# A decoder block with product-key experts: gathered rows for 224 tokens instead of 192, routing four heads at a time, squares of finished rows in SBUF

## The chip, the cores and the metric

The kernel runs on one NeuronCore of a Trainium2 chip, in one launch. The metric is the device time of that launch in microseconds (us). The kernel before took 3629.07 us (median of three runs, 3625.85 to 3631.55). A difference below about 0.2% (some 7 us) can hardly be told from none.

The engines are named as the profile names them: PE multiplies matrices, PEld is its weight load, DVE and ACT work on tiles elementwise, POOL (GpSimd) issues the indirect DMAs, SP issues the plain DMAs. A DMA of either kind runs on the core's 16 DMA engines.

## The reference

512 tokens of width 2048 pass a mixer (a projection to 10240 columns, a short convolution, stick-breaking attention, two gates, an output projection), and then an expert layer, in which the work around the change lies:

```python
q = einsum("btd,dq->btq", rmsnorm(x), wq).reshape(b, t, 8, 2, 128)
scores = einsum("bthsc,snc->bthsn", q, subkeys)         # 8 heads, 2 halves, 128 keys
top_s, top_i = top_k(scores, 16)
cand_s = top_s[..., 0, :, None] + top_s[..., 1, None, :]
cand_i = top_i[..., 0, :, None] * 128 + top_i[..., 1, None, :]
sel_s, sel_pos = top_k(cand_s, 16); sel_i = take_along_axis(cand_i, sel_pos)
act = gelu(einsum("td,thkd->thk", x, u[sel_i])) * softmax(sel_s)
out = rmsnorm(x + einsum("thk,thkd->td", act, v[sel_i]))
```

Each token chooses 8 x 16 = 128 of 16384 experts, and u and v have one row of 2048 floats (8 KB) for each expert.

## The kernel before

The tokens are handled in two halves of 256. For each half come the mixer (`mixer`, `outproj`), normalization and transposition (`chain`) and the scores (`queries`, in two halves of four heads each). Every weight comes from memory in pieces of 128x1024 floats (`whalf`): SP issues its load, ACT rounds it to `whi`, DVE subtracts to get `wlo` (L133, L134), and three matmuls use the pair (`mm3`, L164 to L166). So each piece costs DVE one `wlo`, and two pieces are one unit of the loops that follow.

The expert layer is done in two ways at once.

- **Dense.** For the last ND = 320 tokens `dense` multiplies all 16384 experts: `up` (uT, 128 units) and `down` (vT, 128 units), in 16 chunks of eight units each. Unwanted experts have gate 0; `gates` makes the gate planes. A dense unit is 48 matmuls with 320 columns, 12288 of them in all. The first eight chunks of `up` come first, then eight chunks of `down`, then both in turn.
- **Gathered.** For the first G0 = 192 tokens `gather_tile` fetches rows of u and v: one round is one indirect DMA of 128 rows (1 MB) into a `row` buffer and one DVE pass over 128x2048 (L696 for u, L703 for v). The first 128 tokens take 128 rounds for u and 128 for v. The next 64 tokens lie twice on the 128 partitions, half of the slots each, so they take 64 and 64, and their two partial sums are added at the end (`finish`, L757, L758). There are four `row` buffers (`ROWS`), shared with other work; while v is summed, the sum holds one of them.

`pump` hands out the rounds along the units of PE's work: at rates of about one per unit at first, and in the dense part so that they run out ten units before its end (`even`, L1038). The generator `route` (top 16 of the scores, candidates, gates) is likewise spread over units, by the costs that it yields. When the scores of all eight heads of the first 128 tokens have been routed, the gathering starts (L972).

This is only the order in which the program is written. The Tile scheduler then places every instruction on its engine by a timeline of its own; the engines take their instructions strictly in the order that results. DVE's gather passes keep their order among themselves (`PIN`, L691) and may be put late between the `wlo` of the weights.

A finished 128-token tile gets its norm in `finish_rows`: two squares of 1024 columns, written to a PSUM tile of the same pool as the accumulators of `down` (`rms_scale`, L193), then the scale and the store. The last chunk of `down` transposes its results through PSUM (`tr`, one buffer) in 24 steps, adds them to rows of x (L845), and the final norm follows (L888 to L897). The `row` buffers for those rows are asked for when the gathering is over (L877 to L882).

## Time and profile before

| what | value |
|---|---|
| runs, median (lowest to highest) | 3629.07 us (3625.85 to 3631.55) |
| the profiled execution: span | 3629.1 us, nothing else is listed around it |
| PE busy, share of the span | 3535.7 us, 97% |
| DVE | 2833.4 us, 78% |
| ACT | 1621.6 us, 45% |
| POOL | 644.8 us, 18% |
| data moved | 1056.10 MB, mean 291 GB/s |
| PE's share of the chain that ended last | 73% |

The busy shares are means over stages with different limits, so the stretches of the program have to be read one by one: the columns of the windows below give each engine's busy time in a stretch with the number of its instructions, then PE's granted clock, the busy share of the DMA engines and the rate that they moved.

### The profile page before, as it was taken

How to read it: one execution, taken by the hardware profiler on the slowest of the kernel's cores; microseconds unless marked ns; L12 is line 12 of the kernel's file. 1: busy time of each engine (PE TensorE's matmuls, PEld its weight loads, DVE VectorE, ACT ScalarE, POOL GpSimd, SP SyncE). 2: the span in 40 equal slices, each digit the busy share in tenths (PEclk: the TensorE clock that was granted, in tenths of full speed). 3: DMA queues.
4: the chain of work that ended last, by engine and by line, in shares of the span. 5: the costliest groups of instructions: out<-in, count | busy, mean ns of one | idle time of the engine just before them, and what ended most of it. 6: DMA issues, size and time to landing. Idle time of an engine off the chain costs nothing.

```text
span 3629.1 us, 63343 instructions
## 1 busy us (share of the span) xinstructions
PE 3535.7 (97%) x25347; PEld 3420.6 (94%) x25347; DVE 2833.4 (78%) x4022; ACT 1621.6 (45%) x2277; POOL 644.8 (18%) x520
## 2 busy tenths in 40 slices
PE   9999999999999999889999999999999999999998
PEld 8999999798888999779999999999999999999997
DVE  6555557558988888788999886888887888888885
ACT  5444445445545543554337773333333333333334
POOL 0000000000234222012121111221122322322220
PEclk9999999999999999999999999999999999999998
DMA  5556666663788899899889889899988988889884
GB/s 194 170 176 219 214 216 216 198 193 127 267 306 332 335 344 356 313 331 344 295 324 334 309 317 364 326 358 337 341 328 327 358 328 336 325 338 349 326 319 150
DMA packets 297815, 1056.10 MB, mean 291 GB/s; under 512 B 36464, under 2 KB 109296, under 8 KB 243568
## 3 DMA queue, kind: packets, MB, share of 16 engines
q1 hardware_dynamic: 242224, 649.38, 51.3%
q0 software_dynamic: 55296, 402.68, 28.9%
q8 instruction: 199, 3.26, 0.3%
q14 instruction: 96, 0.79, 0.1%
HBM read 999.98 MB, written 51.38 MB: 290 GB/s over the span
## 4 chain that ended last, share of the span: by engine, by line
PE 73%; DVE 3%; DMA 2%; issue 2%; ACT 1%; POOL 0%; SPq 0%; DVEq 0%; ACTq 0%; POOLq 0%
PE pj L166 13%; PE pj L164 13%; PE pj L165 13%; PE z L164 9%; PE z L165 9%; PE z L166 9%; PE pj L668 2%; DVE wlo L134 1%; PE z L434 1%; PE tr L416 1%; DVE row L696 1%; DMA wraw<-in_w_mix 1%; DMA row<-in_u,idx 1%; PE z L397 0%; DMA gt<-gd 0%
## 5 line engine op out<-in xcount | busy, mean ns | idle before, releaser
L133 ACT ACTIVATE whi<-wraw 128x1024 fp32r<-128x1024 f32 x827 | 874.2, 1059 | 1229.3 <-PE pj L165 726.4
L134 DVE TENSOR_TENSOR wlo<-wraw,whi 128x1024 fp32r<-128x1024 f32 x827 | 1009.2, 1224 | 415.3 <-ACT whi L133 409.5
L166 PE MATMUL pj<-xhi,wlo 128*128 128x256 f32 x2560 | 719.7, 282 | 11.3 <-DVE wlo L134 11.1
L164 PE MATMUL pj<-xhi,whi 128*128 128x256 f32 x2560 | 721.6, 282 | 6.7 <-ACT whi L133 4.7
L165 PE MATMUL pj<-xlo,whi 128*128 128x256 f32 x2560 | 720.5, 282 | 0.0
L164 PE MATMUL pj<-dxhi,whi 128*128 128x320 f32 (+1 forms) x2304 | 710.0, 308 | 2.8 <-ACT whi L133 2.6
L166 PE MATMUL pj<-dxhi,wlo 128*128 128x320 f32 (+1 forms) x2304 | 704.1, 307 | 4.5 <-DVE wlo L134 4.5
L165 PE MATMUL pj<-dxlo,whi 128*128 128x320 f32 (+1 forms) x2304 | 705.8, 307 | 0.0
L164 PE MATMUL z<-ahi,whi 128*128 128x320 f32 x2048 | 631.0, 309 | 4.0 <-ACT z L193 2.9
L165 PE MATMUL z<-alo,whi 128*128 128x320 f32 x2048 | 631.5, 309 | 2.4 <-DVE alo L134 2.4
L166 PE MATMUL z<-ahi,wlo 128*128 128x320 f32 x2048 | 629.6, 309 | 1.8 <-DVE wlo L134 1.8
L166 PEld LDWEIGHTS pj<-xhi,wlo 128*128 128x128 f32 x2560 | 480.0, 188 | 21.5 <-DVE wlo L134 16.1
L164 PEld LDWEIGHTS pj<-xhi,whi 128*128 128x128 f32 x2560 | 481.7, 188 | 12.6 <-ACT whi L133 6.1
L165 PEld LDWEIGHTS pj<-xlo,whi 128*128 128x128 f32 x2560 | 481.4, 188 | 6.7 <-issue 5.3
L685 POOL DMA_INDIRECT row<-in_v,idx x192 | 286.7, 1493 | 1063.8 <-DVE row L703 448.9
L703 DVE SCALAR_TENSOR_TENSOR row<-row,gact 128x2048 f32<-128x2048 f32 x192 | 450.5, 2346 | 19.3 <-DMA row<-in_v,idx 19.3
L696 DVE SCALAR_TENSOR_TENSOR row<-row,gx 128x2048 f32<-128x2048 f32 x192 | 438.4, 2287 | 26.0 <-DMA row<-in_u,idx 25.0
L685 POOL DMA_INDIRECT row<-in_u,idx x192 | 290.8, 1515 | 857.8 <-DVE row L696 213.0
L166 PEld LDWEIGHTS pj<-dxhi,wlo 128*128 128x128 f32 x2304 | 433.3, 188 | 5.6 <-DVE wlo L134 5.6
L164 PEld LDWEIGHTS pj<-dxhi,whi 128*128 128x128 f32 x2304 | 434.5, 189 | 3.2 <-ACT whi L133 2.9
L165 PEld LDWEIGHTS pj<-dxlo,whi 128*128 128x128 f32 x2304 | 434.2, 188 | 0.0
L133 ACT ACTIVATE whi<-spare 128x1024 fp32r<-128x1024 f32 x197 | 208.8, 1060 | 414.8 <-PE z L165 263.8
(232 smaller groups left out, 5019.3 us busy)
## 6 DMA issues: line engine op xcount, KB each, us to landing
wraw<-in_w_in SPq DMA_DIRECT2D x320, 512.0 KB
wraw<-in_uT SPq DMA_DIRECT2D x187, 512.0 KB
wraw<-in_vT SPq DMA_DIRECT2D x128, 512.0 KB
spare<-in_vT SPq DMA_DIRECT2D x128, 512.0 KB
spare<-in_uT SPq DMA_DIRECT2D x69, 512.0 KB
wraw<-in_w_mix SPq DMA_DIRECT2D x64, 512.0 KB
wraw<-in_w_out SPq DMA_DIRECT2D x64, 512.0 KB
wraw<-in_wq SPq DMA_DIRECT2D x64, 512.0 KB
```

The costliest lines, as they stand in the source:

```text
L133: nc.scalar.activation(hi, src, AF.Copy)
L134: nc.vector.tensor_tensor(lo, src, hi.bitcast(F32), OP.subtract)
L164: nc.tensor.matmul(acc, shi, mhi, start=first, stop=False)
L165: nc.tensor.matmul(acc, shi, mlo, start=False, stop=False)
L166: pe_last[0] = nc.tensor.matmul(acc, slo, mhi, start=False, stop=last)
L416: nc.tensor.matmul(yps[hs, q0:], kv[j // 2][1][:, j % 2, hs], e[:, seg(j)], start=j == 0, stop=j == last, skip_group_check=True)
L434: nc.tensor.matmul(z[:, c], stat.bitcast(F32), src[:, c], start=False, stop=True, skip_group_check=True)
L668: behind(nc.tensor.matmul(gp[:, t * P:t * P + P], oh[:, t, 0], oh[:, t, 1], start=True, stop=True))
L685: ins = nc.gpsimd.indirect_dma_start(out=g, out_offset=None, in_=tab, in_offset=bass.IndirectOffsetOnAxis(ap=idx[0:np_, s:s + 1], axis=0))
L696: pin(nc.vector.scalar_tensor_tensor(g, g, 1.0, gx, OP.mult, OP.mult, accum_out=hid[:, s:s + 1]))
L703: pin(nc.vector.scalar_tensor_tensor(acc[0:np_], g, act[:, s:s + 1], acc[0:np_], OP.mult, OP.add))
```

## The change

The gathered tokens become 224 and the dense ones 288. The 96 tokens of the second tile are gathered in two parts: 64 tokens twice on the partitions, as before, and then 32 tokens four times (32 rounds for u, 32 for v), whose four partial sums are added in two steps. Routing works on four heads at a time, in the order tile 0, tile 1, tile 0, tile 1; the gathering starts when the first four heads of tile 0 are done. The squares of finished rows are eight passes of 256 columns with an SBUF tile for the unused output. Line numbers of the kernel after are some 2 to 17 higher.

```diff
-NG2 = 64
+SEGS = ((0, 0, 128), (1, 0, 64), (1, 64, 32))
+NG2 = 96
@@ rms_scale
-        ss = pool.tile([P, 2], F32, name="ss", bufs=2)
-        for c in range(2):
-            junk = ztile()
-            nc.scalar.activation(junk, x[:, c * 1024:c * 1024 + 1024], AF.Square, accum_out=ss[:, c:c + 1])
-        return rms_inv(ss)
+        ss = pool.tile([P, 8], F32, name="ss", bufs=2)
+        for c in range(8):
+            junk = pool.tile([P, 256], F32, name="junk", bufs=1)
+            nc.scalar.activation(junk, x[:, c * 256:c * 256 + 256], AF.Square, accum_out=ss[:, c:c + 1])
+        nc.vector.tensor_reduce(ss[:, 0:1], ss, AX.X, OP.add)
+        return rms_root(ss)
@@ route
-    def route(pool, tile_no, st):
-        ls = pool.tile([P, 2, 8, 2, 16], F32, name="ls", bufs=1)
+    def route(pool, tile_no, hh, st):
+        hs = slice(4 * hh, 4 * hh + 4)
+        ls = pool.tile([P, 2, 4, 2, 16], F32, name="ls", bufs=1)
...
+        if tile_no * P < G0:
+            ef = pool.tile([P, 64], F32, name="fa", bufs=1)
+            nc.vector.scalar_tensor_tensor(ef, flat[:, 0, fs], 128.0, flat[:, 1, fs], OP.mult, OP.add)
+            idx = late[1].tile([P, 64], I32, name=f"idx_{hh}", bufs=2)
+            nc.vector.tensor_copy(idx, ef)
+            st["idx"][tile_no].append(idx)
@@ gather_tile
+                while s // idx[0].shape[1] >= len(idx):
+                    yield
@@ gather
+        for tile_no, p0, n in SEGS:
+            R = P // n
+            rows = slice(tile_no * P + p0, tile_no * P + p0 + n)
...
+            def load_acc(t):
+                if R > 1:
+                    nc.vector.memset(t, 0.0)
+                nc.sync.dma_start(t[0:n], x2d[rows])
+
+            def finish(t):
+                m = P // 2
+                while m >= n:
+                    o = row()
+                    nc.sync.dma_start(o[0:m], t[m:2 * m])
+                    nc.vector.tensor_tensor(t[0:m], t[0:m], o[0:m], OP.add)
+                    m //= 2
+                finish_rows(t, rows, final_gain())
@@ pump, routing, background
-    rounds = 2 * P + (2 * (P // (P // NG2)) if NG2 else 0)
+    rounds = sum(2 * n for _, _, n in SEGS)
-        for tt in range(2):
-            yield from route(rts[0], 2 * h + tt, st)
+        for hh in range(2):
+            for tt in range(2):
+                yield from route(rts[0], 2 * h + tt, hh, st)
-        due = min(due, 0.0) + (SIDE_A0 if not st["routes"][0] else SIDE_A if unit < GATES_AT else SIDE_G)
+        due = min(due, 0.0) + (SIDE_A0 if not st["idx"][0] else SIDE_A if unit < GATES_AT else SIDE_G)
-        if st["routes"][0] and what != "half":
+        if st["idx"][0] and what != "half":
```

What the scheduler makes of this stands in the order of each engine's instructions. First DVE, in the last two chunks of the dense part, where the kernel before ends its gathering; `row<-row,gact` is a round of v, `row,hid<-row,gx` one of u, `wlo` a piece of weights, `hd`, `ahi`, `alo` expert activations, and L758 adds the two partial sums.

```order
L703 SCALAR_TENSOR_TENSOR row<-row,gact 128x2048
L134 TENSOR_TENSOR wlo<-spare,whi 128x1024
L774 TENSOR_TENSOR hd<-hd,gt 128x320
L703 SCALAR_TENSOR_TENSOR row<-row,gact 128x2048
L134 TENSOR_TENSOR wlo<-wraw,whi 128x1024
L134 TENSOR_TENSOR alo<-hd,ahi 128x320
L134 TENSOR_TENSOR wlo<-spare,whi 128x1024
L774 TENSOR_TENSOR hd<-hd,gt 128x320
L134 TENSOR_TENSOR alo<-hd,ahi 128x320
L758 TENSOR_TENSOR row<-row 64x2048
L134 TENSOR_TENSOR wlo<-wraw,whi 128x1024
L197 TENSOR_TENSOR ss<-ss 128x1
```

Behind the last round there 17 `wlo` follow before the program ends. The same engine in the kernel after, at the last `wlo` of the program (L136 there; L854 is the addition of a product of `down`, L773 adds partial sums):

```order
L136 TENSOR_TENSOR wlo<-wraw,whi 128x1024
L708 SCALAR_TENSOR_TENSOR row,hid<-row,gx 128x2048
L854 TENSOR_TENSOR dacc<-z,dacc 128x576
L708 SCALAR_TENSOR_TENSOR row,hid<-row,gx 128x2048 x2
L854 TENSOR_TENSOR dacc<-z,dacc 128x576
L708 SCALAR_TENSOR_TENSOR row,hid<-row,gx 128x2048 x6
L765 MEMSET row 128x2048
L708 SCALAR_TENSOR_TENSOR row,hid<-row,gx 128x2048
L712 TENSOR_TENSOR gact<-gact,gate_34114 128x32
L715 SCALAR_TENSOR_TENSOR row<-row,gact 128x2048 x32
L773 TENSOR_TENSOR row<-row 64x2048
L773 TENSOR_TENSOR row<-row 32x2048
```

The 24 final steps follow these rows. So 42 rounds, ten of u and all 32 of v of the last part, stand behind the last `wlo`, and 39 of them behind the last addition of a product; counted over the dense part, 271 rounds stand among its 512 `wlo`, where 267 stood before.

Second PE at its end, before: `z` are products of `down`, `tr` are transposes.

```order
L166 MATMUL z<-ahi,wlo 128x320
L843 MATMUL tr<-ident,dacc 64x128 x2
L164 MATMUL z<-ahi,whi 128x320
L165 MATMUL z<-alo,whi 128x320
L166 MATMUL z<-ahi,wlo 128x320
```

And after:

```order
L166 MATMUL z<-ahi,whi 128x288
L167 MATMUL z<-alo,whi 128x288
L168 MATMUL z<-ahi,wlo 128x288
L859 MATMUL tr<-ident,dacc 128x128 x4
L859 MATMUL tr<-ident,dacc 32x128 x2
```

Before, 13 of the 24 steps' transposes stand among the products of the last chunk; after, all 24 stand behind the last product.

Third DVE where the gathering starts, before (MAX, MAX_INDEX and MATCH_REPLACE are routing):

```order
L546 MAX ls<-ttmp 128x8 x2
L547 MAX_INDEX ls<-ls,ttmp 128x8 x2
L696 SCALAR_TENSOR_TENSOR row,hid<-row,gx 128x2048
L545 MATCH_REPLACE ttmp<-ls,row 128x128 x2
L403 SCALAR_TENSOR_TENSOR row<-z,row 128x896
```

And after:

```order
L409 SCALAR_TENSOR_TENSOR row<-z,row 128x896
L708 SCALAR_TENSOR_TENSOR row,hid<-row,gx 128x2048
L551 MATCH_REPLACE ttmp<-sv,spare 128x64 x2
L435 TENSOR_TENSOR sums<-row,sums 128x256
L136 TENSOR_TENSOR wlo<-wraw,whi 128x1024
```

Counted in `wlo`, the first round stands behind the 289th piece of weights before and the 268th after; by the 320th there are 19 rounds before and 33 after, by the 512th (the start of the dense part) 117 and 135.

## Rows read from the trace of the kernel before

**Rows 1.** The page: busy time of the engines.
```profile
PE 3535.7 (97%) x25347; PEld 3420.6 (94%) x25347; DVE 2833.4 (78%) x4022; ACT 1621.6 (45%) x2277; POOL 644.8 (18%) x520
```

**Rows 2.** Stretches: from:to, length, busy time by engine, clock, DMA share, GB/s.
```profile
460.00:480.00 20.00, 20.00 (x172) 20.00 (x171) 11.65 (x15) 8.69 (x11) 0.00 (x0) 1.00 0.66 198
797.50:1051.20 253.70, 243.29 (x1792) 216.87 (x1790) 223.92 (x569) 136.31 (x161) 51.20 (x56) 1.00 0.64 223
1716.00:1954.00 238.00, 234.62 (x1605) 233.82 (x1604) 233.29 (x564) 106.76 (x157) 47.41 (x31) 0.99 0.87 313
1954.00:2238.00 284.00, 279.66 (x1998) 278.87 (x1997) 226.29 (x438) 183.46 (x378) 43.36 (x33) 0.99 0.90 331
2238.00:2697.00 459.00, 453.71 (x3073) 450.58 (x3073) 391.13 (x369) 159.23 (x185) 91.93 (x65) 1.00 0.92 339
2697.00:2812.00 115.00, 112.13 (x765) 111.87 (x764) 92.57 (x84) 43.65 (x54) 25.28 (x17) 1.00 0.88 331
2812.00:3489.00 677.00, 677.00 (x4615) 676.58 (x4614) 555.41 (x507) 238.65 (x290) 186.63 (x113) 1.00 0.89 336
3489.00:3605.00 116.00, 115.96 (x796) 115.47 (x795) 84.20 (x93) 47.64 (x78) 9.50 (x7) 1.00 0.64 232
3605.00:3630.00 25.00, 6.53 (x24) 2.50 (x22) 11.88 (x32) 9.48 (x28) 0.00 (x0) 0.57 0.32 105
```

**Rows 3.** PE's timeline: the first and the last dense matmul (start, length).
```profile
1716.40 0.31 PE L164 MATMUL pj<-dxhi,whi 128*128 128x320 f32 x1
...
3604.86 0.31 PE L166 MATMUL z<-ahi,wlo 128*128 128x320 f32 x1
```

**Rows 4.** The page's costliest groups: busy, mean ns, idle before and its releaser.
```profile
L164 PE MATMUL z<-ahi,whi 128*128 128x320 f32 x2048 | 631.0, 309 | 4.0 <-ACT z L193 2.9 <-DVE dacc L838 0.7
L703 DVE SCALAR_TENSOR_TENSOR row<-row,gact 128x2048 f32<-128x2048 f32 x192 | 450.5, 2346 | 19.3 <-DMA row<-in_v,idx 19.3
L696 DVE SCALAR_TENSOR_TENSOR row<-row,gx 128x2048 f32<-128x2048 f32 x192 | 438.4, 2287 | 26.0 <-DMA row<-in_u,idx 25.0 <-DVE wlo L134 1.0
```

**Rows 5.** Stretches in which the DMA engines were fullest.
```profile
2200.00:2250.00 50.00, 46.24 (x304) 45.72 (x303) 35.32 (x36) 18.16 (x26) 10.17 (x7) 0.97 1.00 374
1250.00:1450.00 200.00, 196.11 (x1645) 194.14 (x1644) 163.03 (x174) 81.91 (x102) 44.07 (x30) 1.00 0.95 349
```

**Rows 6.** POOL's timeline: two issues of a gather.
```profile
1069.08 0.97 POOL L685 DMA_INDIRECT row<-in_u,idx  x1 [5.15 <-issue]
...
1111.94 1.68 POOL L685 DMA_INDIRECT row<-in_u,idx  x1 [6.92 <-DVE row L696]
```

**Rows 7.** DVE's timeline: the passes over those two gathers.
```profile
1075.67 2.29 DVE L696 SCALAR_TENSOR_TENSOR row<-row,gx 128x2048 f32<-128x2048 f32 x1 [6.66 <-DMA row<-in_u,idx]
...
1119.26 2.29 DVE L696 SCALAR_TENSOR_TENSOR row<-row,gx 128x2048 f32<-128x2048 f32 x1 [0.85 <-DMA row<-in_u,idx]
```

**Rows 8.** SP's and DVE's timelines: adding the partial sums, then scaling the finished rows.
```profile
3536.68 0.48 SPq L757 DMA_DIRECT2D row<-row  x1
...
3542.09 2.28 DVE L758 TENSOR_TENSOR row<-row 64x2048 f32<-64x2048 f32 x1
...
3550.28 2.35 DVE L725 SCALAR_TENSOR_TENSOR row<-row,ss 128x2048 f32<-128x2048 f32 x1
```

**Rows 9.** DVE's timeline: steps of the final rows once PE's products are done.
```profile
3614.30 0.42 DVE L845 TENSOR_TENSOR row<-tr,row 128x256 f32<-128x256 f32 x1
...
3615.69 0.41 DVE L845 TENSOR_TENSOR row<-tr,row 64x256 f32<-64x256 f32 x1
...
3618.85 0.41 DVE L845 TENSOR_TENSOR row<-tr,row 128x256 f32<-128x256 f32 x1
```

More of the change, by code (lines that the diff above doesn't have):

```diff
@@ L547, in top16 @@
         nc.vector.max_index(ti[:, 8:16], tv[:, 8:16], tmp)
-    def route(pool, tile_no, st):
-        ls = pool.tile([P, 2, 8, 2, 16], F32, name="ls", bufs=1)
+    def route(pool, tile_no, hh, st):
+        hs = slice(4 * hh, 4 * hh + 4)
+        ls = pool.tile([P, 2, 4, 2, 16], F32, name="ls", bufs=1)
         tv, ti = ls[:, 0], ls[:, 1].bitcast(U32)
-        for _ in range(8):
+        for _ in range(4):
             while not st["topk"][tile_no]:
@@ L728, in gather @@
     def gather(routes):
-        idx = routes[0][0]
-        yield from gather_tile(
-            late[1], P, P, idx, st["gate"],
-            lambda t: nc.sync.dma_start(t, xn2d[0:P]),
-            lambda t: nc.sync.dma_start(t, x2d[0:P]),
-            lambda t: finish_rows(t, slice(0, P), final_gain()))
-        if not NG2:
-            return
-        S = P // (P // NG2)
-        idx, eg = routes[1]
-        idx2 = late[1].tile([P, S], I32, name="idx2")
-        gate2 = late[1].tile([P, S], F32, name="gate2")
@@ L741, in gather @@
-        for r in range(P // NG2):
-            ps_, ss = slice(r * NG2, r * NG2 + NG2), slice(r * S, r * S + S)
-            nc.sync.dma_start(idx2[ps_], idx[0:NG2, ss])
-            nc.sync.dma_start(gate2[ps_], eg[0:NG2, 2, ss])
-        def load_x(t):
-            for r in range(P // NG2):
-                nc.sync.dma_start(t[r * NG2:r * NG2 + NG2], xn2d[P:G0])
-        def load_acc(t):
-            nc.vector.memset(t, 0.0)
-            nc.sync.dma_start(t[0:NG2], x2d[P:G0])
-        def finish(t):
-            for r in range(1, P // NG2):
-                o = row()
-                nc.sync.dma_start(o[0:NG2], t[r * NG2:r * NG2 + NG2])
-                nc.vector.tensor_tensor(t[0:NG2], t[0:NG2], o[0:NG2], OP.add)
-            finish_rows(t, slice(P, G0), final_gain())
@@ L761, in gather, with load_x @@
-        yield from gather_tile(late[1], P // NG2 * NG2, S, idx2, gate2, load_x, load_acc, finish)
+        for tile_no, p0, n in SEGS:
+            R = P // n
+            rows = slice(tile_no * P + p0, tile_no * P + p0 + n)
+            idx, gate = st["idx"][tile_no], st["gate"]
+            if R > 1:
+                src, eg = routes[tile_no]
+                idx = [late[1].tile([P, n], I32, name=f"idx{n}")]
+                gate = late[1].tile([P, n], F32, name=f"gate{n}")
+                for r in range(R):
+                    ps_, ss = slice(r * n, r * n + n), slice(r * n, r * n + n)
+                    c = r * n % 64
+                    nc.sync.dma_start(idx[0][ps_], src[r * n // 64][p0:p0 + n, c:c + n])
+                    nc.sync.dma_start(gate[ps_], eg[p0:p0 + n, 2, ss])
+            def load_x(t):
+                for r in range(R):
+                    nc.sync.dma_start(t[r * n:r * n + n], xn2d[rows])
+            def load_acc(t):
+                if R > 1:
+                    nc.vector.memset(t, 0.0)
[8 more added lines that the diff above has]
+                finish_rows(t, rows, final_gain())
+            yield from gather_tile(late[1], P, n, idx, gate, load_x, load_acc, finish)
@@ L897, in dense @@
                 nc.sync.dma_start(out[G0 + c:G0 + c + n, half * 1024:half * 1024 + 1024], xs)
-    st = {"routes": [None] * 4}
+    st = {"routes": [None] * 4, "eg": [None] * 4, "idx": [[] for _ in range(4)]}
     credit = 0.0
```

81 lines of the change are left out of this document (41 added, 40 removed).

## The prediction

> **What bounds the kernel now.** I read the page's busy times first, then the stretches, then the timelines at the end. PE is busy 3535.7 of 3629.1 us [rows 1], and the stretches show that this is no average over mixed stages: from 2812 to 3489 us PE is busy for all of 677 us at granted clock 1.00, while DVE has 555 of 677 and the DMA engines 0.89 [rows 2]. There only PE can set the time, and a change that shortens its matmuls is paid out until the next engine is full. How near that engine is differs by stretch: DVE has 233.3 of 238 us from 1716 to 1954, and the DMA engines 0.92 from 2238 to 2697 [rows 2]. The dense part lasts from 1716.4 to 3604.9 us [rows 3], and after the last product only 24.2 us are left to the end at 3629.1. The profiled span equals the median of the runs (3629.07) within 0.1 us, so the sum is made on the span and not scaled.
>
> **Dense matmuls, the gain.** A matmul with 320 columns takes 677 / 4615 = 146.7 ns from start to start, one with 256 columns 20.00 / 172 = 116.3 ns [rows 2]. 288 lies half way: 131.5 ns, 15.2 ns less. 12288 of them make 187 us: 47 in the first 3072 (1716 to 2238), 47 in the next (2238 to 2697), 93 in the rest. What of it is kept depends on the neighbours. DVE's order has almost as many rounds per piece of weights as before (271 in the dense part against 267), so DVE's and the DMA engines' work stays nearly what it is and has to fit into less time.
>
> - 1716 to 2238: in the first half DVE is busy 233.3 of 238 us, and routing of the other tokens, one-hot planes and 63 rounds against 62 are still its work. I grant 3 us there. In the second half (DVE 226 of 284) PE's 24 us are free. Sum -27, bounds 0 and -47.
> - 2238 to 2697: the DMA engines moved 339 GB/s x 459 us = 155.6 MB, and nearly the same must be moved. The best 50 us of the trace have 374 GB/s at a full share of 1.00 [rows 5]; at that rate it takes 416 us, PE would need 412. DVE, busy 391 us now, loses only a tenth of its passes over 320 and 640 columns, and would stand at some 380 of 412 (an estimate). Two engines so near to full do not fit without gaps; I take 423 us, -36, bounds -10 and -47.
> - The rest, 2697 to 3605: 115 x 331 + 677 x 336 + 116 x 232 = 292.5 MB; at 374 GB/s 782 us, and PE needs 907 - 93 = 814. From 1250 to 1450 us PE kept 98% beside a DMA share of 0.95 [rows 5], so little is lost. PE's 4.0 us of waits at the products of `down`, 2.9 of them for the squares in PSUM [rows 4], go with the SBUF tile (-3), and the 13 pairs of transposes that leave the last chunk, 26 at about the 116 ns of a narrow matmul, give -3 here and come back below. -99 at best; I take -88, bound -60.
>
> The Trainium skill, *DMA: Bandwidth & Descriptors* (Specifications), gives about 358 GB/s as a core's share of the memory. The 374 GB/s over 50 us above exceed it, so I do not use it as a wall; by it the second stretch would take 435 us and the sum below come out 12 us higher. The same skill's *TensorE: Matmul & The Clock Gate* (Back-to-back issue gap) has N / 2.4 + 2.5 ns per matmul, 135.8 for 320 columns, where the rows have 146.7; by the page the step to 288 is worth 13.3 ns, an estimate 24 us lower in all and some 12 us after the stretches' own limits.
>
> **Before the dense part, a loss.** From 797 to 1051 us DVE is busy 223.9 of 253.7 us and PE 243.3 [rows 2]. By the order, 33 rounds instead of 19 now stand before the 320th `wlo`: 14 x (2.29 + 0.08) = 33 us more for DVE. Routing in half-width pieces doubles some 22 small instructions per tile (+5), and some of routing moves behind the 320th `wlo` (-5). 257 us no longer fit into 253.7; at 97% busy it takes 265: +12 us, bounds -4 (all of it finds gaps, and 32 tokens fewer need planes) and +33. The DMA engines have room there (0.64). The start of gathering cannot help by itself: what stands behind it is paced by PE's units.
>
> **Behind the last product, the new cost.** Here the order decides, not the pacing in the program. Before, the last round has 17 `wlo` behind it, so the addition of the partial sums, the norm and 13 of the 24 final steps lie beside products. After, the scheduler has put 42 rounds behind the last `wlo`, 39 of them behind the last addition of a product, and all 24 final steps behind those. PE is done by then and hides nothing. Step by step:
>
> - 7 rounds of u at 2.37 us [rows 4] and a memset: 19 us.
> - 32 rounds of v. One buffer's cycle is issue to pass, 1075.67 - 1069.08 = 6.6 and 1119.26 - 1111.94 = 7.3 us [rows 6, 7], two cases in which DVE waited for the data, and the pass itself, 2.35 [rows 4]: 9.0 to 9.7. Three of the four buffers are left beside the sum, so 3.0 to 3.2 us a round. DVE alone would need 2.35 (75 us in all); two buffers only, 4.7 (150). The weights no longer load, so I take 3.0: 96 us.
> - Two additions of partial sums, each behind its own DMA: before, at most 3542.09 - 3536.68 = 5.4 us from the issue to the addition, and 2.28 for that [rows 8]. At most 15; I take 13.
> - From the end of the addition to the scaling it was 3550.28 - 3544.4 = 5.9 us, and 2.35 for the scaling [rows 8]: 8.
> - The rows of x for the 128-row steps need buffers that are free only now. Loading 1 MB costs about what a gather does (6.6 to 7.3 [rows 6, 7]); the second waits for the store as well: 8, bounds 4 and 12.
> - 21 more steps at 3615.69 - 3614.30 = 1.39 us, the pace with nothing beside them (the granted clock of these 25 us is 0.57, that is, partly at the lower of the two levels) [rows 2, 9]: 29. From the start of the last step to the end, 3629.1 - 3618.85 = 10.
>
> Together 183 us (bounds 155 and 240) where 24 stand now. DVE's queue is strict, so every final step waits behind the 32 rounds; POOL's and SP's have nothing else left by then.
>
> Edits that I cost at nothing in the dense part: eight squares instead of two on ACT (45% busy, rows 1), hidden by PE's products, some 2 us if bare (in the 8 above, once); the two half-size index tiles; the earlier index copies on SP.
>
> **Sum.** 3604.9 + 12 - 27 - 36 - 88 = 3466 for the last product, + 183 = 3649, say 3650 us: slower by 0.6%. A difference of 0.2% is about what can be told from none, 7 us here.
>
> **Rivals.**
>
> *PE collects everything.* DVE and the DMA engines fill their gaps (0.99 and 0.95 with PE near full do occur [rows 2, 5]): -47, -47, -99 and nothing lost ahead of it. 3604.9 - 193 + 183 = 3595 us. It turns the sign once the last product comes more than 166 us earlier (183 - 24 + 7). For it: rows of late stretches with PE at 100%. Against: the first half of 1716 to 2238, where DVE has 5 us left. 0.13.
>
> *The neighbours keep half.* Two nearly full engines wait for each other in turn; only half of 187 us is paid: 3604.9 + 12 - 94 + 183 = 3706. For it: from 797 to 1051 PE already lost 10 us at DVE 88%. Against: the full PE beside DMA 0.89. 0.15.
>
> *Gain and tail cancel.* The v rounds run at DVE's own 2.35 to 2.5 us, because the DMA engines serve them alone: the tail is about 165, the time 3632, no difference. For it: the weights are over. Against: three buffers and 6.6 us of latency. 0.12.
>
> *The rounds go as the program paces them,* not as the order stands: the last 252 of the 448 in the last 197 units, some 1.4 a unit towards the end, no tail. It would need (1 + 1.4) x 1.05 + 0.07 = 2.6 MB per unit of 6.3 us, 412 GB/s, above the 374 seen; at 374 a unit takes 6.95 us against 7.04 now, and the time is about 3600. The order excludes it but for an error of mine: 0.02.
>
> **Numbers.** The forecast itself has 0.58, its own range 3622 to 3690. Faster by over 0.2% (below 3621.8): 0.15 (PE collects everything 0.13, paced rounds 0.02). Within: 0.12. Slower: 0.58 + 0.15 = 0.73. The range reaches into both outer cases: 3603 to 3708.
>
> **What would show it.** Right: in the changed kernel's stretches the last dense matmul ends near 3466 us, PE is nearly idle for some 180 us after it with the clock falling, POOL and DVE alternate there in 32 passes about 3.0 us apart, and then 24 final steps stand alone. Dense matmuls are 131 ns apart where PE is full. Wrong: if the last product ends before 3440, the neighbours cost less than I think; if the passes of the tail are 2.4 us apart, my buffer cycle is wrong; if PE waits for `wlo` in the late chunks too, the loss is in the dense part and not behind it.

## The result, and the profile after

The changed kernel takes 3759.65 us (median of 4 runs, 3751.54 to 3763.23) where the kernel before takes 3630.31 on the same chip: ratio 1.0346, 95% interval 1.0325 to 1.0367. I had said 3650, with a range up to 3708: the sign is right, the size is outside the range. The profiled execution of after has a span of 3761.4 us, 132.3 more than before.

The page's busy times answer [rows 1]: PE has 126 us less, DVE 129 more.

```profile
PE 3409.4 (91%) x25283; PEld 3270.9 (87%) x25283; DVE 2962.8 (79%) x4186; ACT 1623.9 (43%) x2291; POOL 740.0 (20%) x584
```

PE's timeline gives the borders, as [rows 3] did: the first dense matmul, and the last.

```profile
1746.19 0.40 PE L166 MATMUL pj<-dxhi,whi 128*128 128x288 f32 x1 [1.03 <-ACT whi L135]
...
3567.75 0.29 PE L168 MATMUL z<-ahi,wlo 128*128 128x288 f32 x1
```

So the 132.3 us are +29.8 ahead of the dense part, -66.9 in it (1821.6 us against 1888.5) and +169.4 behind it (193.6 against 24.2). I had +12, -151 and +159. The tail came as forecast; the dense part paid 67 us of the 151.

The stretches, with the columns of [rows 2] and cut at the same places of the work (the 257th and 320th `wlo`, the dense part's start, its first 3072 up products in two pieces, the first 3072 down products, the next 48 units of 48 products, the last 80, the tail):

```profile
799.00:1061.00 262.00, 244.19 (x1770) 218.29 (x1769) 251.28 (x608) 130.52 (x154) 76.48 (x69) 0.98 0.75 274
1061.00:1746.00 685.00, 636.88 (x4548) 585.63 (x4546) 542.05 (x703) 311.53 (x396) 163.09 (x130) 0.96 0.88 326
1746.00:1978.00 232.00, 215.97 (x1597) 212.88 (x1598) 224.57 (x524) 100.55 (x137) 58.70 (x31) 0.97 0.85 306
1978.00:2272.00 294.00, 271.38 (x2049) 267.61 (x2049) 235.28 (x468) 193.25 (x404) 54.82 (x34) 0.97 0.90 324
2272.00:2711.00 439.00, 419.04 (x3077) 411.98 (x3076) 386.41 (x383) 162.67 (x204) 97.58 (x67) 0.99 0.95 357
2711.00:3048.00 337.00, 315.65 (x2305) 311.27 (x2304) 287.36 (x289) 120.01 (x146) 92.86 (x61) 0.98 0.95 357
3048.00:3568.00 520.00, 510.95 (x3843) 509.27 (x3842) 436.06 (x390) 203.43 (x257) 118.08 (x83) 1.00 0.90 337
3568.00:3761.00 193.00, 15.33 (x47) 5.52 (x46) 122.17 (x113) 21.87 (x73) 56.92 (x37) 0.51 0.66 243
```

Two things are to be seen. Only from 3048 us on is PE full again (510.95 of 520); there the narrower matmuls are paid out. From 2272 to 3048 PE, DVE and the DMA engines stand at 0.94 to 0.95, 0.85 to 0.88 and 0.95 together, and the transfers run at 357 GB/s in both stretches. And in the tail PE has 15 us of 193.

DVE's waits say what is late in the second half of the up products (1978 to 2272 us): the gathered rows.

```profile
DVE row L715 <- DMA row<-in_v,idx: 46.9, 17, 7.8
```

In the corresponding stretch of before (1954 to 2238 us) the same wait was 18.6 us:

```profile
DVE row L703 <- DMA row<-in_v,idx: 18.6, 11, 4.1
```

And PE's own waits: the group of `down` products that needs `wlo`, before and after, with the idle time in front of it as the last figures.

```profile
L166 PE MATMUL z<-ahi,wlo 128*128 128x320 f32 x2048 | 629.6, 309 | 1.8 <-DVE wlo L134 1.8
L168 PE MATMUL z<-ahi,wlo 128*128 128x288 f32 x2048 | 602.6, 296 | 24.4 <-DVE wlo L136 24.2
```

In the groups of the products of `up`, which hold 256 others too, PE waited 15.1 us for `wlo` (4.5 before) and 20.2 for `whi` (2.6 before).

The tail on DVE's timeline: one pass of `v` with its wait and the last two (L715), the two additions of partial sums (L773), the scaling (L739), and two of the final steps (L861).

```profile
3603.21 2.35 DVE L715 SCALAR_TENSOR_TENSOR row<-row,gact 128x2048 f32<-128x2048 f32 x1 [3.25 <-DMA row<-in_v,idx]
...
3689.49 4.75 DVE L715 SCALAR_TENSOR_TENSOR row<-row,gact 128x2048 f32<-128x2048 f32 x2 [0.58 <-DMA row<-in_v,idx]
3698.48 2.28 DVE L773 TENSOR_TENSOR row<-row 64x2048 f32<-64x2048 f32 x1 [4.25 <-DMA row<-row]
3703.88 2.28 DVE L773 TENSOR_TENSOR row<-row 32x2048 f32<-32x2048 f32 x1 [3.11 <-DMA row<-row]
...
3712.32 2.35 DVE L739 SCALAR_TENSOR_TENSOR row<-row,ss 128x2048 f32<-128x2048 f32 x1
...
3720.35 0.42 DVE L861 TENSOR_TENSOR row<-tr,row 128x256 f32<-128x256 f32 x1 [5.36 <-DMA row<-x2d]
...
3750.58 0.40 DVE L861 TENSOR_TENSOR row<-tr,row 128x256 f32<-128x256 f32 x1
```

The 32 passes over `v` lie between 3592.83 and 3694.2 us, 3.17 us each, most of them behind a wait for their row.

### The profile page after: what moved, and what is told of

It reads as the page before. It is cut to its first block, busy times and chain, and to the rows that moved or that the text cites. A ratio compares the mean times of both kernels' runs of the same rounds, so it can differ in the third digit from the quotient of the medians.

```text
span 3761.4 us, 63562 instructions
## 1 busy us (share of the span) xinstructions
PE 3409.4 (91%) x25283; PEld 3270.9 (87%) x25283; DVE 2962.8 (79%) x4186; ACT 1623.9 (43%) x2291; POOL 740.0 (20%) x584
## 5 line engine op out<-in xcount | busy, mean ns | idle before, releaser
L136 DVE TENSOR_TENSOR wlo<-wraw,whi 128x1024 fp32r<-128x1024 f32 x827 | 1006.5, 1222 | 328.7 <-ACT whi L135 325.3
L166 PE MATMUL pj<-dxhi,whi 128*128 128x288 f32 (+1 forms) x2304 | 688.3, 299 | 22.8 <-ACT whi L135 20.2
L168 PE MATMUL pj<-dxhi,wlo 128*128 128x288 f32 (+1 forms) x2304 | 686.0, 299 | 15.3 <-DVE wlo L136 15.1
L167 PE MATMUL pj<-dxlo,whi 128*128 128x288 f32 (+1 forms) x2304 | 675.7, 294 | 0.0
L168 PE MATMUL z<-ahi,wlo 128*128 128x288 f32 x2048 | 602.6, 296 | 24.4 <-DVE wlo L136 24.2
L166 PE MATMUL z<-ahi,whi 128*128 128x288 f32 x2048 | 607.6, 298 | 11.9 <-ACT ahi L135 7.7
L167 PE MATMUL z<-alo,whi 128*128 128x288 f32 x2048 | 607.1, 297 | 3.0 <-DVE alo L136 3.0
L715 DVE SCALAR_TENSOR_TENSOR row<-row,gact 128x2048 f32<-128x2048 f32 x224 | 525.6, 2346 | 81.7 <-DMA row<-in_v,idx 75.5
L697 POOL DMA_INDIRECT row<-in_v,idx x224 | 347.0, 1549 | 1133.2 <-DVE row L715 554.5
L708 DVE SCALAR_TENSOR_TENSOR row<-row,gx 128x2048 f32<-128x2048 f32 x224 | 510.9, 2286 | 40.1 <-DMA row<-in_u,idx 40.1
L168 PEld LDWEIGHTS z<-ahi,wlo 128*128 128x128 f32 x2048 | 388.4, 190 | 29.6 <-DVE wlo L136 29.5
```

What stands on the lines that cost most here:

```text
L136: nc.vector.tensor_tensor(lo, src, hi.bitcast(F32), OP.subtract)
L166: nc.tensor.matmul(acc, shi, mhi, start=first, stop=False)
L167: nc.tensor.matmul(acc, shi, mlo, start=False, stop=False)
L168: pe_last[0] = nc.tensor.matmul(acc, slo, mhi, start=False, stop=last)
L697: ins = nc.gpsimd.indirect_dma_start(out=g, out_offset=None, in_=tab, in_offset=bass.IndirectOffsetOnAxis(ap=idx[s // w][0:np_, s % w:s % ...
L708: pin(nc.vector.scalar_tensor_tensor(g, g, 1.0, gx, OP.mult, OP.mult, accum_out=hid[:, s:s + 1]))
```

## The experiments

Each kernel is told by its difference to the changed kernel. One table holds the readings of all (first dense matmul; length of the dense part, and in it the first 3072 up products, the next 3072 down products and the rest; tail; time). Where an interval is given, the ratio to the kernel before was timed in three rounds; the others were timed once. The runs e9 and e13 have two thirds of the products, so their columns are cut at 2048 up and 2048 down products. The runs e2, e5, e6, e9 and e10 leave out work of the expert sums, e13 the low half of the tokens in the dense products; they show where time goes and are no kernels to use.

```
kernel                      first   dense    up   down   rest   tail   time    ratio
before                     1716.4  1888.5   522   459    908   24.2   3630
changed                    1746.2  1821.6   526   439    857  193.6   3760  1.0346 [1.0325, 1.0367]
e1 192 tokens              1753.8  1893.5   535   454    904   24.4   3675  1.0117 [1.0100, 1.0134]
e2 no third part           1739.4  1765.0   520   423    822   47.9   3556  0.9789 [0.9773, 0.9805]
e3 old start               1718.2  1808.0   517   433    858  237.9   3766  1.0368 [1.0351, 1.0385]
e4 order held at 2         1801.6  1951.9   527   472    953   30.6   3798  1.0460 [1.0442, 1.0478]
e5 an eighth fetched       1722.6  1786.6   495   446    846   31.6   3543
e6 an eighth passed        1705.8  1769.3   481   430    858  186.1   3663
e7 order held at 12        1742.8  1899.9   524   446    930   67.4   3708  1.0193 [1.0169, 1.0216]
e8 208 tokens              1752.2  1861.1   528   449    885   73.8   3692  1.0175 [1.0144, 1.0205]
e9 two products, 1/8 pass  1710.7  1611.4   455   393    763  189.2   3513
e10 light gathers          1684.4  1694.9   473   409    813   30.0   3411
e11 more landing           1741.3  1786.9   519   454    814  273.0   3802  1.0456 [1.0431, 1.0482]
e12 held at 12, landing    1732.7  1887.4   513   455    919   65.4   3696  1.0175 [1.0158, 1.0192]
e13 two products           1751.5  1737.7   504   409    825  205.4   3696
```

**e1, routing and early start alone.** 192 gathered tokens and 320 dense columns as before; the squares stay in PSUM.

```diff
-SEGS = ((0, 0, 128), (1, 0, 64), (1, 64, 32))
-NG2 = 96
+SEGS = ((0, 0, 128), (1, 0, 64))
+NG2 = 64
```

(Not shown: the lines that put the squares back into PSUM.)

> The changed routing and its early start alone: 192 gathered tokens as before (128 whole, 64 twice on the partitions), 320 dense columns, squares in PSUM as before. Theory A (the early rounds overload DVE before the dense part): the first dense matmul stays at about 1746 us, 30 later than before, and as 18 rounds less are left for the dense part, the end is about 3645 us. Rival (the early start is harmless, the late first dense matmul comes from the wider index tiles and the third part's transfers): first dense matmul at 1716 to 1722, the end at 3625.

Measured 3675: slower than both theories, and slower than before by 1.2%. The dense part begins 37 us later, its first up products take 13 us longer, and what follows wins back 9. The 18 rounds more that stand ahead of it by the order buy little later, since a unit behind the first down products takes 7.04 to 7.08 us (7.09 to 7.11 before), which is PE's own time at 320 columns. So the new routing and its early start alone lose over 40 us, a third of the whole loss.

**e2, without the third part.** The 32 tokens of it get no expert sum, only norm and store: 384 rounds beside 288 columns.

```diff
-    rounds = sum(2 * n for _, _, n in SEGS)
+    rounds = sum(2 * n for _, _, n in SEGS[:2])
```

(Not shown: in `gather` the third part then only loads, norms and stores its 32 rows.)

> The changed kernel without the 64 rounds of the third part (its 32 tokens get no expert sum, only norm and store); dense stays at 288 columns. Theory A (narrow matmuls are paid out as long as there is about one round per dense unit): first dense matmul at 1746, the dense part about 1725 us long (187 less than before, some 25 lost), no tail beyond 30 us, in all 3500 us. Rival (at 288 columns the weights alone fill DVE and the DMA engines, rounds or not): the dense part stays near the 1822 us of the changed kernel, in all 3595 us.

Measured 3556, between the two. The third part's 64 rounds cost 3760 - 3556 = 204 us, 3.2 us a round (by the profiled executions 146 in the tail, 57 in the dense part, 7 ahead of it). The 288 columns are worth 128 us of dense time against e1 (1765.0 to 1893.5), and 119 of the whole, as the tail is longer. That is the change in one line: routing and early start lose some 40 us, the columns give 119 instead of 187, and the rounds take 204.

**e3, start and routing order as before.** Routing in half-width pieces stays, but tile by tile, and gathering starts with the whole first tile.

```diff
-        for hh in range(2):
-            for tt in range(2):
+        for tt in range(2):
+            for hh in range(2):
-        if st["idx"][0] and what != "half":
+        if st["routes"][0] and what != "half":
```

> The changed kernel with routing tile by tile and the gathering started when all eight heads of tile 0 are routed, as before. The order of DVE then has 123 rounds at the start of the dense part (135 in the changed kernel, 117 before) and 56 behind the last piece of weights (42). Theory A (early start costs 30 us before the dense part, each round behind the last product costs 3.1 us): first dense matmul at 1725, the dense part as in the changed kernel, a tail 45 us longer, in all 3780 us. Rival (the 30 us come from half-width routing or the 64 further rounds, not from the start): first dense matmul at 1746, in all 3800 us.

Measured 3766, below both theories (3780 and 3800). The dense part begins at 1718.2, only 2 us behind before: so the half-width pieces by themselves cost next to nothing, and the early start, with the order of routing that goes with it, costs 28 us; the two were not taken apart. Giving them up returns nothing on balance: 14 more rounds now stand behind the last `wlo`, and the tail is 44.3 us longer, 3.16 us for each. Ahead of the last product the same 14 rounds had cost 28.0 + 13.6 = 41.6 us, 3.0 each if all of it is put down to them.

**e4 and e7, rounds as the program paces them.** Each `wlo` is put in DVE's order behind the pass that is 2 (e4) or 12 (e7) rounds before the program's own place.

```diff
+        if len(passes) > HOLD:
+            tc.add_manual_dep(sub.ins, passes[-1 - HOLD].ins.name, mybir.DependencyInfo(mybir.DependencyClass.NoSync, mybir.DependencyReason.DATA), reason="hold")
```

(Not shown: the split of a piece, written out so that `sub` is its subtraction, and the list `passes` of the gather passes so far.)

> The changed kernel with every subtraction of a piece of weights held behind the third last gather pass that the program has handed out, so that DVE's order follows the program's pacing: 271 rounds in the dense part become 313, none stands behind the last piece of weights. Theory A (the tail is a matter of the order, and in the dense part DVE and the DMA engines limit): the tail falls from 194 to about 25 us, the dense part grows from 1822 to 1900 us, since 1.4 rounds a unit move 2.6 MB that take 6.9 us at 374 GB/s; in all 3670 us. Rival (PE has room for the rounds, only their place was bad): the dense part stays at 1822, in all 3590 us.

> The changed kernel with each low half of a weight piece held in DVE's order behind the gather pass that is twelve rounds before the program's own place, so that the rounds go as the program paces them (1.4 a unit at the end, one round behind the last weight piece) while DVE still has weight pieces in hand. Theory A (the rounds cost the same wherever they stand, since the dense part has no room for more than one a unit): the tail of 194 us shrinks to about 45 and the dense part grows by about as much, 3740 to 3770 us. Theory B (the order of the scheduler is the loss, the dense part could hold them): about 3620 us.

e4 took 3798, far above both theories (3670 and 3590). Its tail is gone, but `wlo` now has no lead: the dense part begins 55 us later than in the changed kernel, and from 2700 to 3700 us PE waits 70 us for `wlo`, and DVE in turn 55 us for PE's sums. That is a test of a DVE without lead, not of the pacing. e7 leaves twelve rounds of lead and took 3708, between its two theories: the tail shrinks by 126 us, the dense part grows by 78, and 52 us are won against the changed kernel. So the scheduler's order is about two fifths of the loss of 129 us. Of the other part, 1.4 rounds a unit do not fit beside PE: a unit with 1.39 rounds (the last 80) takes 7.22 us, more than the 7.09 of before. Put there, a round costs some 2 us (78 us for the 39 that stood behind the last product), in the tail over 3. Over e7's last 6144 products (the line's columns are those of [rows 2]) no engine has much left:

```profile
2712.00:3643.00 931.00, 849.90 (x6151) 837.36 (x6150) 801.59 (x721) 323.88 (x404) 268.94 (x176) 0.97 0.93 355
```

**e5, e6 and e10, the two costs of a round apart.** e5 fetches 256 of a row's 2048 columns and passes over 2048; e6 fetches all and passes over 256; e10 does both.

The fetch of e5 and e10:

```diff
-            ins = nc.gpsimd.indirect_dma_start(out=g, out_offset=None, in_=tab, in_offset=bass.IndirectOffsetOnAxis(ap=idx[s // w][0:np_, s % w:s % w + 1], axis=0))
+            ins = nc.gpsimd.indirect_dma_start(out=g[:, 0:256], out_offset=None, in_=tab.rearrange("r (c d) -> (r c) d", c=8), in_offset=bass.IndirectOffsetOnAxis(ap=idx[s // w][0:np_, s % w:s % w + 1], axis=0))
```

(Not shown: e5's passes, which keep their length, 2.29 and 2.35 us.) The `v` pass of e6 and e10 (the `u` pass likewise):

```diff
-            pin(nc.vector.scalar_tensor_tensor(acc[0:np_], g, act[:, s:s + 1], acc[0:np_], OP.mult, OP.add))
+            pin(nc.vector.scalar_tensor_tensor(acc[0:np_, 0:256], g[:, 0:256], act[:, s:s + 1], acc[0:np_, 0:256], OP.mult, OP.add))
```

> The changed kernel, but each gather fetches 256 of the 2048 columns of a row (128 KB instead of 1 MB a round); DVE's passes keep their 2048 columns: the u pass multiplies the token rows by themselves, the v pass reads the 256 columns eight times. The expert sums are therefore not the reference's. By the order all 448 rounds stand ahead of the last weight piece (1.4 a unit at the end), so there is no tail. Theory A (DVE's passes are what the dense part waits for): first dense product still near 1746 us, its first 3072 products 526 us, the next 435, the rest about 6.9 us a unit (883), 25 behind it: about 3615 us. Theory B (the DMA engines are): first dense product near 1746, then 505, 410 and 6.4 us a unit (819): about 3505 us, granted clock near 0.99.

> The changed kernel, but DVE's gather passes work on 256 of the 2048 columns (the fetches stay whole), so the expert sums are not the reference's. By the order 44 rounds still stand behind the last weight piece. Both theories: the first dense product comes 15 to 30 us sooner than 1746, because DVE is what is full there. Theory A (DVE bounds the dense part): 490 us, 410 us and 6.4 us a unit (815) after that, tail about 190: near 3630 us. Theory B (the DMA engines bound it): 520, 437, 850, tail about 190: near 3720 us. In the tail B expects the passes to stay 3.1 to 3.2 us apart, as fetches set the pace there by both theories.

> The changed kernel with both costs of a round relieved: an eighth fetched and 256 of 2048 columns passed, so the expert sums are not the reference's. PE has all its products. Both theories: no gathers in its way, PE's 131.5 ns a product is paid in full from the first down product on (406 us, then 6.34 us a unit, 812), the first 3072 products near 470, the first of them near 1695, 25 behind the last: about 3410 us at a granted clock of 0.99. Were it the scheduler's order or the routing that holds the dense part back, it would stay above 3480.

e6's stretches of the first down products and of the 48 units behind them:

```profile
2187.00:2617.00 430.00, 417.66 (x3072) 413.95 (x3071) 267.14 (x373) 164.33 (x204) 74.57 (x63) 0.98 0.96 359
2617.00:2956.00 339.00, 317.01 (x2309) 313.06 (x2309) 178.10 (x294) 118.57 (x146) 75.39 (x62) 0.97 0.95 354
```

The same two in e5:

```profile
2219.00:2664.00 445.00, 421.28 (x3073) 417.36 (x3074) 412.09 (x408) 162.97 (x204) 168.04 (x78) 0.97 0.65 216
2664.00:2984.00 320.00, 310.31 (x2306) 307.78 (x2305) 297.55 (x280) 119.33 (x146) 128.38 (x68) 0.99 0.61 202
```

And in e10, with the last 80 units as a third row:

```profile
2157.00:2566.00 409.00, 406.93 (x3075) 405.58 (x3074) 268.11 (x400) 163.10 (x202) 106.66 (x78) 1.00 0.70 234
2566.00:2871.00 305.00, 305.00 (x2310) 305.00 (x2310) 180.63 (x281) 121.76 (x147) 89.75 (x69) 1.00 0.63 212
2871.00:3379.00 508.00, 508.00 (x3850) 507.86 (x3850) 311.36 (x438) 211.29 (x290) 140.34 (x100) 1.00 0.62 209
```

e10 took 3411 us where 3410 was expected: with both costs gone PE is full at clock 1.00, and 288 columns are paid out whole, 6.35 us a unit, 132 ns a matmul. e5 took 3543 and e6 3663, each between its two theories (3505 and 3615, 3630 and 3720). Ahead of the dense part DVE's passes matter most (e6 begins 40 us sooner, e5 24), and in the up products both do (45 and 31 us). Split at the 1537th of the 3072 up products, the changed kernel takes 242 and 284 us, e6 216 and 265, e5 235 and 260, e10 212 and 261: the first half is held by the passes, the second more by the fetches. From 2272 to 3048 us neither theory holds by itself. With light passes the time hardly moves (430 and 339 against 439 and 337), though DVE is busy for only 267 and 178 us of it, and the transfers stay at 354 to 359 GB/s; with light fetches 1.4 rounds a unit stand in the order, and DVE is nearly full (412 of 445, 298 of 320). In e6's tail the passes still wait for their rows, as DVE's timeline shows:

```profile
3573.47 0.48 DVE L715 SCALAR_TENSOR_TENSOR row<-row,gact 128x256 f32<-128x256 f32 x1 [1.94 <-DMA row<-in_v,idx]
...
3590.11 0.48 DVE L715 SCALAR_TENSOR_TENSOR row<-row,gact 128x256 f32<-128x256 f32 x1 [1.98 <-DMA row<-in_v,idx]
```

These are the first and the last of seven, on average 2.77 us apart; over all 32 passes of that tail it is 2.79 us each, against 3.17 in the changed kernel. The stretches of these passes, first the changed kernel's, then e6's in two pieces:

```profile
3594.00:3694.00 100.00, 0.00 (x0) 0.00 (x0) 73.97 (x32) 0.00 (x0) 40.27 (x29) 0.50 0.82 305
3500.00:3559.00 59.00, 0.00 (x0) 0.00 (x0) 9.21 (x19) 0.00 (x0) 18.16 (x19) 0.50 0.93 334
3559.00:3593.00 34.00, 0.00 (x0) 0.00 (x0) 6.24 (x13) 0.00 (x0) 9.37 (x10) 0.50 0.90 348
```

**e8, 208 tokens.** 16 tokens in the third part, 304 columns, 416 rounds. The pacing ends 40 units ahead of the end of the dense part instead of 10 (`DRAIN`), so two things change at once.

```diff
-SEGS = ((0, 0, 128), (1, 0, 64), (1, 64, 32))
+SEGS = ((0, 0, 128), (1, 0, 64), (1, 64, 16))
-DRAIN = 10
+DRAIN = 40
```

> The changed kernel with 208 gathered tokens and 304 dense columns: the third part has 16 tokens, so 416 rounds instead of 448, and the pacing ends 40 units ahead of the end instead of 10; by the order two rounds stand behind the last weight piece. Theory (a round costs 2.4 to 3.2 us from about one a unit on, a matmul of 304 columns 139 ns): first dense product near 1743, its last near 3567, tail 55: about 3622 us, ratio 0.997 to the kernel before. Rival (each round beyond the 384 of before costs its 3 us in full, and PE's 93 us are paid in half only, as in the changed kernel): about 3680 us.

Measured 3692, the rival's side. Half the step costs about half: 57 us over before, against 129 for the whole.

**e9 and e13, PE relieved.** The dense part leaves out the product with the tokens' low half, a third of its matmuls; e9 has the 256-column passes as well.

```diff
-        nc.tensor.matmul(acc, shi, mlo, start=False, stop=False)
+        if mhi.shape[-1] != ND:
+            nc.tensor.matmul(acc, shi, mlo, start=False, stop=False)
```

> The changed kernel with two relieved engines: DVE's gather passes work on 256 of 2048 columns, and the dense part leaves out one of its three products (the tokens' low half), so PE needs 1077 instead of 1615 us there. All transfers stay. Expert sums are not the reference's. Theory B (from some 357 GB/s on, the DMA engines are the limit, whatever PE and DVE do): the 2048 down products of the first chunks take 425 to 432 us (154 MB at 357 to 360 GB/s, as in the run with passes of 256 columns: 430), the 48 units behind them 330 to 339, the last 80 units 485 to 495 instead of 519 (174 MB), all at a share of 0.94 to 0.97. Rival (357 GB/s is only what three busy engines in turn leave; alone the transfers reach 374 or more, the best 50 us of before): 413 us or less, 320, 466.

> The changed kernel without one of the three dense products (the tokens' low half, so the dense result is coarser), 1077 instead of 1615 us of PE work; passes and fetches of the gathers stay whole, and the rounds stand where the changed kernel has them (44 behind the last weight piece). Theory D (no engine is the limit by itself there; PE, DVE and the DMA engines, each near 0.95, hold each other up through few buffers): with PE relieved the first down products take 400 to 415 us instead of 439 at 375 GB/s or more, the next 48 units 310 to 320 instead of 337, and DVE comes to 0.93 or more. Rival E (DVE's passes keep the transfers at 357 GB/s, PE is not concerned): 430 to 440 and 330 to 340 as before, at a DMA share of 0.95. The last 80 units take 480 to 500 by D, 515 to 520 by E. The first 3072 up products stay near 526 by both, half of them beside a full DVE. Tail 194.

e9's stretches of the first down products and the 48 units behind them:

```profile
2165.00:2559.00 394.00, 315.53 (x2052) 300.54 (x2050) 264.94 (x377) 160.12 (x205) 76.66 (x64) 0.92 1.01 397
2559.00:2862.00 303.00, 240.44 (x1536) 230.96 (x1536) 175.19 (x291) 116.95 (x146) 73.63 (x61) 0.89 1.02 399
```

The same in e13, and its last 80 units:

```profile
2255.00:2664.00 409.00, 320.74 (x2051) 306.55 (x2051) 378.33 (x380) 160.03 (x206) 107.03 (x64) 0.89 0.98 373
2664.00:2994.00 330.00, 246.08 (x1538) 235.49 (x1537) 288.99 (x293) 118.90 (x146) 84.19 (x62) 0.88 0.97 371
2994.00:3489.00 495.00, 397.70 (x2562) 387.72 (x2561) 436.97 (x388) 199.46 (x257) 156.96 (x83) 0.87 0.92 353
```

e9 tells against theory B: 397 and 399 GB/s over 697 us, at a share that the profile gives as full (1.01 and 1.02), so 357 is no wall of the memory. In e13, with PE alone relieved, the down products take 409 us at 373 GB/s (theory D's 400 to 415), the 48 units 330 (rival E's 330 to 340, though at 371 GB/s) and the last 80 units 495 (D's 480 to 500). The first up products took 504 us where both expected 526, and the tail 205 where 194 was expected. PE and the transfers hold each other up in the down products; in the 48 units DVE and the transfers do so too, more than D allowed.

**e11 and e12, more landing buffers.** SPB2 is 5 instead of 3 and the pieces are dealt out over all nine buffers in turn; e12 holds the order at 12 as well.

```diff
-SPB2 = 3
+SPB2 = 5
-        if spare_ok[0] and turns[0] % 2:
+        if spare_ok[0] and turns[0] * SPB2 % (SPB2 + WRAW) < SPB2:
```

> The changed kernel with nine instead of seven landing buffers for weight pieces from the first down product on (SPB2 5 instead of 3, the pieces dealt out over both pools in turn). By the order 64 instead of 42 rounds stand behind the last weight piece. Theory C (with PE, DVE and the DMA engines all near 0.95, the loads wait for buffers that DVE frees late, and more of them let the transfers run closer to the 397 GB/s seen with PE relieved): the 3072 down products of the first chunks take 410 to 425 us instead of 439, the rest 820 (0.95 rounds a unit), the tail 194 + 22 x 3.17 = 264: about 3760 us. Rival (buffers are not it; PE, DVE and DMA engines share something else): 436 to 440 us for the down products, rest 825, tail 264: about 3785 us.

> The changed kernel with both: rounds held to the program's pace as in e7 and nine landing buffers from the first down product on. Same places of the rounds as in e7 (one behind the last weight piece). Theory C: the down products 415 to 430 instead of 446, the rest some 870 instead of 931, tail 67: about 3630 us, no difference to the kernel before. Rival (buffers are not it): as e7, 3700 to 3715 us.

Theory C falls. e11's down products take 454 us instead of 410 to 425, longer than the rival's 436 to 440 too (PE waits there 26.7 us for `ahi` on ACT, 7.7 in the changed kernel), and the whole 3802 where C had 3760 and the rival 3785. e12 is 12 us below e7 where C wanted 80, and the intervals of the two ratios overlap. The rest of e11 takes 814 us with PE full: the order leaves 22 more rounds for the tail, 273 us, and 123 instead of 145 for the rest; e2, with 128 there and the buffers unchanged, takes 822. No kernel of this study with all its work is below the kernel before.

## Why the prediction was wrong, point by point

The sum said 3649 us, the profiled execution took 3761.4. Of the 112 us between them 84 lie in the dense part, 18 ahead of it and 10 behind it. The step that failed is the overlap in the dense part: that in the second half of the first up products "PE's 24 us are free", and that beside transfers near full only some 2% over the longest engine are lost. There 67 us were won instead of 151. What the runs show in its place: the stretches in which another engine needs as long as PE take 5 to 11% more than the longest engine, and PE waits for weight pieces, 24.2 us for `wlo` at the products of `down` where it was 1.8. That PE waits for `wlo` in the late chunks had been named as a sign that the loss is in the dense part, and it came: 14.8 us in the 48 units, 7.6 in the last 80.

**The product's size was right.** 131.5 ns was the estimate; e10 has 132, and the changed kernel 520 / 3843 = 135 ns from 3048 us on.

**Ahead of the dense part: mis-sized.** +12 (bounds -4 and +33) became +29.8. The stretch up to the 320th `wlo` grew by 8 us, near the 12 reckoned; the other 20 come from there to the first dense matmul, which I had not priced: the prediction says only that what stands behind the start is paced by PE's units. It is not paced by PE alone: with light passes the dense part begins 40 us sooner (e6), with light fetches 24 (e5), with both 62 (e10). The cause is the early start with its order of routing (e3: 28 us), not the half-width pieces (2 us).

**The up products: failed.** -27 became +4. PE alone would have won 49 us against before (e10: 473). My first half was full of DVE as said (224.57 of 232). The step that failed is "in the second half PE's 24 us are free": there DVE waits 46.9 us for gathered rows, and the half took 284 us where it was 281. With light fetches it takes 260, the same as with both costs gone (261): the rows come too late, and the prediction had no price for the transfers in this stretch.

**The down products and the rest: the same error, and the largest.** -36 became -20, -88 became -51. I divided the bytes by 374 GB/s, the best 50 us of before [rows 5], and took 2% over that, 423 us, for "two engines so near to full"; for the rest I took some 1% over PE, since from 1250 to 1450 us PE had kept 98% beside a DMA share of 0.95. The rate was not too high (e9 shows 397); the 2% was too small. What each engine needs by itself the runs give: for the down products PE 409 us (e10), the transfers 394 (e9), DVE 386 busy; it took 439, 7% over the longest. For the next 48 units PE 305 (e10), the transfers 303 (e9), DVE 287 busy; it took 337, 10% over. For the last 80 units PE 508 (e10), DVE 436, the transfers some 440 (337 GB/s x 520 us at e9's 398, an estimate); 520, 2% over. Before, in the down products, PE needed 3072 x 146.7 ns = 451 us, DVE 391, the transfers some 392 (155.6 MB at 397, an estimate), and it took 459, again 2% over [rows 2].

So 2% holds where the next engine has 86 or 87% of the longest, and 4 to 11% is lost where it is level; the change made them level. It does not take three. In e6 DVE is far from full, and PE (409, 305) and the transfers (394, 303) alone take 430 and 339 us, 5 and 11% over. In e13 PE is relieved, and the transfers and DVE (394 and 378, 303 and 289) take 409 and 330, 4 and 9% over. In e5 the fetches are light, and PE and DVE (409 and 412, 305 and 298) take 445 and 320, 8 and 5% over. DVE as a third adds little (439 against 430, 337 against 339). This is no law: the second half of the up products lost 9% (284 us against the 261 of e10) with the transfers at some 240 (324 GB/s x 294 us at 397, an estimate). The rest fell short in its first 48 units: they won 4 us against before, where the narrower products are worth some 35; the last 80 won 47 of some 58. One reason may be the order, which is argued and not shown: 42 rounds stand beside the 32 units behind the 768th `wlo`, 1.3 a unit, so the rest's bytes are not even.

**The squares.** PE's 2.9 us of waits for them are gone, as forecast; but e1 keeps the squares in PSUM, and PE's idle time before these products is 0.5 us there too. No run changes the squares alone.

The Trainium skill, *DMA: Bandwidth & Descriptors* (Specifications), gave 358 GB/s a core, and by it the down products would have come to 435 us, an estimate; 439 was measured, at 357 GB/s. The agreement misleads: e9 ran at 397. The Trainium skill's *Perfetto Trace Analysis* (Roofline) says why it may, since a core that runs alone can draw more than that share; e9 agrees. By the formula of *TensorE: Matmul & The Clock Gate* (Back-to-back issue gap) in the Trainium skill 288 columns would take 122.5 ns, an estimate, but the section gives the formula for single matmuls and says that in a stream with weight loads in between the spacing is set by both; e10 shows 132.

**The tail: right in size, and in its steps.** 183 (155 to 240) and 193.6 measured. The `v` passes came 3.17 us each against 3.0 to 3.2 from three buffers' cycle; the additions, the scaling and the steps at 1.39 us came within a few us, and a wait of 3.2 us for the rows of x with which the sum starts had not been priced. That the cycle of three buffers is the reason is not shown in full. By e6 the pass is a part of it: with 0.48 us of pass instead of 2.35 a round takes 2.79. But the cycle alone would then give (6.6 + 0.48) / 3 = 2.4 to (7.3 + 0.48) / 3 = 2.6 us, and the DMA engines are at 0.90 to 0.93 there, against 0.82 in the changed kernel, which points at the transfers as well.

**The rivals.** "The neighbours keep half" (3706) had the mechanism, and too small a price: 67 us of the dense part were won, where it had 94. "PE collects everything" is what e10 shows once the gathers are light. "Gain and tail cancel" needed passes 2.35 to 2.5 us apart; they came 3.17 apart. "Rounds as the program paces them" would have been 3600, at 6.95 us a unit with 1.4 rounds; e7 shows 3708, at 7.22.

**What stays open.** By what engines that are level hold each other up, through buffers or otherwise: two more landing buffers, dealt out as in e11 and e12, do not help, and no run gives the halves `whi` and `wlo` more. The granted clock is 0.96 to 0.99 where PE has short waits, against 0.99 to 1.00 in the dense part of before. At 0.99 over 439 us and 0.98 over 337 that is some 4 and 7 us of PE's time (an estimate), of the 30 and 32 over what PE needs; no run takes it apart. In e8's down products the clock is 1.00, and they still take 448 us, at 359 GB/s. The runs e5, e6, e9, e10 and e13 were timed once, so differences of a few us against them say nothing.

## What to carry to other kernels

Add up what each engine needs for the same stretch, from runs that relieve the others where possible. Where a change brings a second engine level with the first, expect a loss over the longest, not the longest alone: here 4 to 11%, against 2% where the second had 86 or 87% of it. Work moved from the bound engine to ones that are 85% busy is not free anywhere: a round cost over 3 us behind the last product, and some 2 us beside PE when it was held to the program's pace (e7). Look in the order of the instructions for what is left behind the last product, before the time of a change is summed up.

## What the runs showed of the hardware that was not expected

The transfers held 397 to 399 GB/s over 697 us (e9), well above the 374 of the best 50 us before. The mean granted clock was lower where PE had pauses, though none of them was long: 0.89 at 320.74 busy of 409 us and 0.87 at 397.70 of 495 (e13, no pause over 6.5 us), that is, partly at the lower of the two levels, against 1.00 at 508 of 508 (e10).
